# A forgetting-attention layer on one core: transposes of q, k and p moved from TensorE to VectorE and ScalarE

## The chip, the cores and the metric

The kernel runs on one core of a Trainium2 chip, in one launch. The metric is the device time of an execution in microseconds (us). An execution's time is a little longer than the span that the profile shows, since something lies before the first and after the last profiled instruction.

Engine names as in the profile: PE is TensorE's matmul, PEld its weight load, DVE VectorE, ACT ScalarE, POOL GpSimd, SP the engine that issues the large DMAs.

## What is computed

One layer, of the kind that the reference calls FoX (a softmax attention with a cumulated forget gate instead of positions), and a gated feed-forward network with a causal convolution of width 3 behind it. The sequence has 256 positions, the model 2048 columns, there are 16 heads of 128, and the feed-forward part has 2 x 5632 columns. Everything is float32. Cut to what matters here:

```python
def fox_mixer(h, w_in, b_f, q_gain, k_gain, w_out):
    q, k, v, f_logit = jnp.split(h @ w_in, [hd, 2 * hd, 3 * hd], axis=-1)
    q = rms_norm(q.reshape(bsz, seq, N_HEADS, HEAD_DIM), q_gain)
    k = rms_norm(k.reshape(bsz, seq, N_HEADS, HEAD_DIM), k_gain)
...
    cum = jnp.cumsum(log_sigmoid(f_logit + b_f), axis=1).transpose(0, 2, 1)
    s = jnp.einsum('bqhd,bshd->bhqs', qb, k) * HEAD_DIM ** -0.5
    s = s + (cq[..., :, None] - cum[:, :, None, :])
    return _causal_softmax(s, start, v)          # then @ w_out

h = h + fox_mixer(rms_norm(h, mix_norm), ...)
h = h + conv_ffn(rms_norm(h, ffn_norm), w_up, conv_w, conv_b, w_down)
```

## The kernel before

**Tiles.** The 256 positions are two tiles of 128 (t), the 2048 model columns 16 k-tiles of 128. Every large product is made of three matmuls per k-tile and t: each operand is split into a high part (hi), which is a cast to the reduced type fp32r, and a low part (lo), the rest; hi*hi, hi*lo and lo*hi are summed (L324 to L326). A matmul of this kind has 512 columns.

**Weights.** `split_load` (L159) brings four k-tiles of 512 columns (1 MB) in one DMA from SP into one of 4 raw buffers; then for each half of it (two k-tiles, 1024 columns) ACT casts the hi tile (L169) and DVE subtracts to make the lo tile (L170). hi and lo have HBUF = 5 buffers each, so a cast can start only when PE has read the tile five before it for the last time. Two k-tiles feed 12 matmuls.

**Attention.** The heads are worked in four groups of four (GROUPS, heads 12 to 15 first). For each group g the chunks q, k and v are made one after the other (`chunk`, L308; in group 0 v is made in two pieces, v0a, which also carries the forget gate's 16 columns, and v0b). Behind a q or k chunk ACT moves the two banks to SBUF with the row's scale (`qk_evac`), DVE squares and sums per head and POOL takes the power -0.5, DVE scales each head (`qk_norm`, L409). Then q and k must be turned, so that the 128 columns of a head lie on the partitions: `qk_turn` (L414) does it with PE, by matmuls against an identity, four 128x128 squares into a bank of PSUM, and ACT copies the bank to SBUF with the gain per partition (L425), into T0 (q) and T1 (k).

**Scores and output of a head.** `scores` (L435) makes the bias on POOL from the cumulated gate (which comes over DRAM, `scr` to `ckB`), two matmuls (sc), adds the bias and takes the maximum on DVE, exponentials with sums on ACT (L463), reciprocal and two scalings on DVE (L469). The result s is p, 128 x 384 per head: positions 0 to 127 see 128 keys, positions 128 to 255 see 256. `turn_p` (L474) turns its three squares with PE (pp, L477) and DVE copies them to pT (L479). `mix_v` (L482) multiplies v with pT into a bank po, ACT casts the hi half os from it and DVE subtracts the lo half.

**What sets the order.** Steps that belong behind a chunk are put into a queue of functions, `bg`; `tick()` takes one from it after every second k-tile of the next chunks. `attend_steps` (L500) hands out one step per tick: in step i the scores of head i, the turn of p of head i - LAG_P (3), the product with v of head i - LAG_V (5). A scheduler then puts the instructions of each engine into one fixed order, and each engine works its own order from the front; an instruction that waits holds all that stand behind it on its engine. After the four groups comes the output projection (`out_part`), whose rows of os it needs, group by group, and the addition to the residual (`out_evac`, L293), whose result is turned again for the feed-forward part (`h_turn`, two steps for each of four column blocks).

Of the kernel before, what the change touches and what calls it, by code (L numbers as in the profile page):

```python
# [9 lines left out]
F32 = mybir.dt.float32  # L10
# [6 lines left out]
S = 256  # L17
NT = S // P
# [11 lines left out]
LAG_P = 3  # L30
LAG_V = 5
# [64 lines left out]
def trunk_kernel(  # L96
# [193 lines left out]
    def out_evac(pts, c):  # L290
        for t in range(NT):
            hc = res[:, t, c * 512 : (c + 1) * 512]
            nc.vector.tensor_tensor(hc, hc, pts[t], op=ALU.add)  # L293
            sq = hp_.tile([P, 512], F32, tag="hsq", name=f"hsq{c}_{t}")
            square(sq, t, c)
        bg.extend([
            nop,
            (lambda kp=2 * c: h_turn(kp)),
            (lambda kp=2 * c + 1: h_turn(kp)),
        ])  # L300

    with tc.tile_pool(name="att", bufs=2) as att, tc.tile_pool(name="ckp", bufs=1) as ckp:
# [110 lines left out]

        def qk_turn(sb, i, nh, grp):  # L414
            tT = att.tile([P, 4, S], F32, tag=f"T{i}", name=f"T{i}_{grp}", bufs=1)

            def pair(hp, w):
                pt = bank(f"pT{i}_{grp}_{hp}")
                for h in range(w):
                    for t in range(NT):  # L420
                        nc.tensor.transpose(
                            pt[:, h * S + t * P : h * S + (t + 1) * P],
                            sb[:, t, (hp + h) * HD : (hp + h + 1) * HD], ident,
                        )
                nc.scalar.activation(  # L425
                    tT[:, hp : hp + w, :],
                    pt[:, 0 : w * S].rearrange("p (h s) -> p h s", s=S),
                    AF.Copy, scale=gqk[i],
                )

            return tT, [
                (lambda hp=hp: pair(hp, min(2, nh - hp))) for hp in range(0, nh, 2)
            ]

        def scores(hh, h, qT, kT, ckB):  # L435
# [17 lines left out]
            s = att.tile([P, 3 * P], F32, tag="s", name=f"s{hh}", bufs=4)  # L453
# [18 lines left out]
            return s  # L472

        def turn_p(hh, s):  # L474
            pp = bank(f"pp{hh}")
            for i in range(3):
                nc.tensor.transpose(pp[:, i * P : (i + 1) * P], s[:, i * P : (i + 1) * P], ident)  # L477
            pT = att.tile([P, 3 * P], F32, tag="pT", name=f"pT{hh}")
            nc.vector.tensor_copy(pT, pp[:, 0 : 3 * P])  # L479
            return pT  # L480

        def mix_v(hh, h, pT, vsb):  # L482
            po = bank(f"po{hh}")
# [15 lines left out]

        def attend_steps(g, h0, nh, qT, kT, vsb):  # L500
            st = {}

            def step(i):
                if i == 0:
                    st["ckB"] = ckB = att.tile([P, 4, S], F32, tag="ckB", name=f"ckB{g}", bufs=1)
                    nc.gpsimd.dma_start(
                        ckB[:, 0:nh, :].rearrange("p h s -> p (h s)"),
                        scr[h0 : h0 + nh, :].rearrange("h s -> (h s)").unsqueeze(0).to_broadcast([P, nh * S]),
                    )
                    return  # L510
                i -= 1
                if 0 <= i - LAG_V < nh:
                    h = i - LAG_V
                    mix_v(h0 + h, h, st["p", h], vsb)
                if 0 <= i - LAG_P < nh:
                    h = i - LAG_P
                    st["p", h] = turn_p(h0 + h, st["s", h])
                if i < nh:
                    st["s", i] = scores(h0 + i, i, qT, kT, st["ckB"])

            return [(lambda i=i: step(i)) for i in range(nh + LAG_V + 1)]

        for g, (h0, nh) in enumerate(GROUPS):
            qd = {}

            def q_done():
# [3 lines left out]
                bg.extend([nop] * max(0, 3 - len(bg)))  # L530
# [32 lines left out]
            bg.extend([nop] * 3)  # L563
# [190 lines left out]
```

## Time and profile before

| what | value |
|---|---|
| median of three timed executions | 1133.18 us (1133.14 to 1133.82) |
| the profiled execution, its own time | 1132.92 us |
| span of that execution in the profile | 1131.2 us |
| PE busy | 1124.5 us, 99% of the span |
| PEld busy | 962.1 us, 85% |
| DVE busy | 737.0 us, 65% |
| ACT busy | 580.4 us, 51% |
| POOL busy | 53.1 us, 5% |
| granted clock of PE, mean | 1.00 |

Busy time counts each moment in which at least one instruction of the engine is under way. Matmuls are pipelined: the next one starts before the one ahead has ended, so the mean duration of one (391 ns for 512 columns) is longer than its share of the time. The time that one really takes is read from rows of the chain, where a run of them has a start and a length. The first transpose of q starts at 57 us of the span and the last po at 333; what follows is the output projection and, for two thirds of the span, the feed-forward part, which the change does not touch but for `h_turn`.

### The profile page before, as it was taken

The numbers are of one execution on the slowest core, as the hardware profiler recorded it, in microseconds if no ns is written. First come the engines' busy times: TensorE is split into PE (matmuls) and PEld (weight loads), VectorE is DVE, ScalarE is ACT, GpSimd is POOL, SyncE is SP. The second block draws the span as 40 slices with busy tenths as digits, with TensorE's granted clock in tenths as the row PEclk, the third lists the DMA queues.
The fourth block names the chain that finished last, engine by engine and source line by source line (L and its number), as shares of the span: only waits on it lengthen the run. The fifth ranks groups of instructions, "written<-read, shape, count | busy, mean of one in ns | idle before, by whom it ended". The sixth has DMA issues, their size and how long they took to land.

```text
span 1131.2 us, 14984 instructions
## 1 busy us (share of the span) xinstructions
PE 1124.5 (99%) x5796; PEld 962.1 (85%) x5796; DVE 737.0 (65%) x1189; ACT 580.4 (51%) x853; POOL 53.1 (5%) x102
## 2 busy tenths in 40 slices
PE   9999999999999999999999999999999999999998
PEld 6898888888888888888888888888888888888886
DVE  7667556566556557777755777775577767547864
ACT  7655454454445456555434555543465554345542
POOL 0104011030100000000000000000000000000000
PEclk9999999999999999999999999999999999999999
DMA  9765454554545555555555555555555555555552
GB/s 345 293 204 207 157 197 154 182 198 156 186 155 186 186 178 184 197 187 186 191 200 183 183 204 192 187 186 193 184 187 198 194 193 193 188 185 186 191 182 75
DMA packets 33543, 215.23 MB, mean 190 GB/s; under 512 B 3824, under 2 KB 4112, under 8 KB 9152
## 3 DMA queue, kind: packets, MB, share of 16 engines
q1 hardware_dynamic: 32624, 211.96, 54.3%
q0 software_dynamic: 704, 2.30, 0.6%
q8 instruction: 45, 0.74, 0.3%
q14 instruction: 26, 0.21, 0.1%
q10 hardware_dynamic: 144, 0.02, 0.0%
HBM read 212.15 MB, written 2.11 MB: 189 GB/s over the span
## 4 chain that ended last, share of the span: by engine, by line
PE 99%; DMA 0%; DVE 0%; SPq 0%; ACT 0%; issue 0%
PE puv L265 14%; PE pug L265 14%; PE puv L267 7%; PE pug L267 7%; PE pd L276 7%; PE pd L278 7%; PE pd L277 7%; PE pk L324 3%; PE pk L326 3%; PE po L276 3%; PE po L278 3%; PE pk L325 3%; PE po L277 3%; PE pq L325 3%; PE pq L326 2%; PE pq L324 2%
## 5 line engine op out<-in xcount | busy, mean ns | idle before, releaser
L265 PE MATMUL pug<-hs,hi_ug 128*128 128x512 f32 x704 | 168.1, 391 | 0.0
L265 PE MATMUL puv<-hs,hi_uv 128*128 128x512 f32 x704 | 167.9, 391 | 0.0
L170 DVE TENSOR_TENSOR lo_ug<-raw_ug,hi_ug 128x1024 fp32r<-128x1024 f32 x88 | 106.0, 1221 | 84.3 <-PE puv L267 39.3
L170 DVE TENSOR_TENSOR lo_d<-raw_d,hi_d 128x1024 fp32r<-128x1024 f32 x88 | 106.6, 1222 | 78.7 <-ACT hi_d L169 56.1
L169 ACT CAST hi_d<-raw_d 128x1024 fp32r<-128x1024 f32 x88 | 92.2, 1052 | 114.8 <-PE pd L278 83.1
L265 PEld LDWEIGHTS pug<-hs,hi_ug 128*128 128x128 f32 x704 | 129.6, 188 | 25.3
L265 PEld LDWEIGHTS puv<-hs,hi_uv 128*128 128x128 f32 x704 | 129.4, 188 | 25.0
L169 ACT CAST hi_ug<-raw_ug 128x1024 fp32r<-128x1024 f32 x88 | 92.5, 1051 | 109.7 <-PE puv L265 37.9
L169 ACT CAST hi_uv<-raw_uv 128x1024 fp32r<-128x1024 f32 x88 | 92.5, 1051 | 100.2 <-PE pug L265 64.0
L170 DVE TENSOR_TENSOR lo_uv<-raw_uv,hi_uv 128x1024 fp32r<-128x1024 f32 x88 | 106.2, 1220 | 57.4 <-PE pug L267 40.6
L277 PE MATMUL pd<-lo_d,gt 128*128 128x512 f32 x352 | 136.2, 389 | 0.0
L276 PE MATMUL pd<-hi_d,gt 128*128 128x512 f32 x352 | 134.5, 389 | 0.0
L278 PE MATMUL pd<-hi_d,gt 128*128 128x512 f32 x352 | 134.2, 389 | 0.0
L267 PEld LDWEIGHTS pug<-hs,lo_ug 128*128 128x128 f32 x704 | 90.3, 191 | 3.4
L267 PEld LDWEIGHTS puv<-hs,lo_uv 128*128 128x128 f32 x704 | 90.3, 191 | 3.4
L267 PE MATMUL puv<-hs,lo_uv 128*128 128x256 f32 x704 | 91.3, 283 | 0.0
L267 PE MATMUL pug<-hs,lo_ug 128*128 128x256 f32 x704 | 91.3, 283 | 0.0
L278 PEld LDWEIGHTS pd<-hi_d,gt 128*128 128x128 f32 x352 | 66.1, 188 | 13.8
L276 PEld LDWEIGHTS pd<-hi_d,gt 128*128 128x128 f32 x352 | 66.1, 188 | 13.6
L277 PEld LDWEIGHTS pd<-lo_d,gt 128*128 128x128 f32 x352 | 66.1, 188 | 13.6
L170 DVE TENSOR_TENSOR lo_o<-raw_o,hi_o 128x1024 fp32r<-128x1024 f32 x32 | 39.2, 1224 | 31.2 <-ACT hi_o L169 31.2
L170 DVE TENSOR_TENSOR lo_q<-raw_q,hi_q 128x1024 fp32r<-128x1024 f32 (+1 forms) x33 | 39.3, 1192 | 28.8 <-ACT hi_q L169 28.7
(169 smaller groups left out, 1820.0 us busy)
## 6 DMA issues: line engine op xcount, KB each, us to landing
raw_ug<-in_w_up SPq DMA_DIRECT2D x44, 1024.0 KB, 4.9
raw_uv<-in_w_up SPq DMA_DIRECT2D x44, 1024.0 KB, 4.9
raw_d<-in_w_down SPq DMA_DIRECT2D x44, 1024.0 KB, 4.9
raw_k<-in_w_in SPq DMA_DIRECT2D x16, 1024.0 KB, 4.9
raw_o<-in_w_out SPq DMA_DIRECT2D x16, 1024.0 KB, 4.9
raw_q<-in_w_in SPq DMA_DIRECT2D x12, 1024.0 KB, 4.9
raw_v<-in_w_in SPq DMA_DIRECT2D x12, 1024.0 KB, 4.8
raw_q<-in_w_in SPq DMA_DIRECT2D x7, 512.0 KB, 6.7
```

The costliest lines, as they stand in the source:

```text
L169: nc.scalar.copy(hi[:, 0 : w * n], src)
L170: nc.vector.tensor_tensor(lo[:, 0 : w * n], src, hi[:, 0 : w * n].bitcast(F32), op=ALU.subtract)
L265: nc.tensor.matmul(o[:, 0:512], lhsT=hv, rhs=a.rearrange("p a s -> p (a s)"), start=first, stop=False)
L267: nc.tensor.matmul(o[:, 0:S], lhsT=lv, rhs=a[:, 0, :], start=False, stop=last)
L276: nc.tensor.matmul(pts[t], lhsT=ah, rhs=hv, start=first, stop=False)
L277: nc.tensor.matmul(pts[t], lhsT=ah, rhs=lv, start=False, stop=False)
L278: nc.tensor.matmul(pts[t], lhsT=al, rhs=hv, start=False, stop=last)
L324: nc.tensor.matmul(o, lhsT=ah, rhs=hv[j], start=(k == 0), stop=False)
L325: nc.tensor.matmul(o, lhsT=ah, rhs=lv[j], start=False, stop=False)
L326: nc.tensor.matmul(o, lhsT=al, rhs=hv[j], start=False, stop=(k == KT - 1))
```

## The change

The line numbers shift by a few.

- **q and k.** The transposes on PE and the copy of a bank are gone. `squares` turns each 128x512 half of q or k in place, in squares of 32x32, with one DVE instruction (STREAM_TRANSPOSE, L419): after it, each square is turned, but still lies in the quarter of the partitions in which it lay before. `move(d)` brings the squares to their places: for each quarter d of the result four ACT copies (L425), one from each quarter o of the partitions, each of 32 partitions by 2 x 4 x 32 elements, with the gain as before. That makes 2 DVE and 16 ACT instructions for a q or k of a group, in five steps of the queue; before there were 16 matmuls and 2 ACT copies of 128x512, in two steps.
- **p.** The transposes on PE and DVE's copy of 128x384 are gone. `turn_p` turns the p of all four heads together, for quarter o of the rows and quarter d of the columns in one STREAM_TRANSPOSE on DVE that reads 32 partitions and writes 32 others (L474, 12 squares of 32x32): 16 instructions for a group, in four steps.
- **The order.** Attention goes by stage: one step fetches the gate's sums, one makes the scores of all four heads, four turn p, and one multiplies all four heads with v. The p and pT of a group are one tile each. A bank po is shared by two heads. The empty steps (`nop`) ahead of the turns go, others come into `attend_steps`. `h_turn` does two of its pieces in one tick.

```diff
...
@@ -295,8 +294,7 @@
             square(sq, t, c)
         bg.extend([
             nop,
-            (lambda kp=2 * c: h_turn(kp)),
-            (lambda kp=2 * c + 1: h_turn(kp)),
+            (lambda c=c: [h_turn(kp) for kp in (2 * c, 2 * c + 1)]),
         ])
 
     with tc.tile_pool(name="att", bufs=2) as att, tc.tile_pool(name="ckp", bufs=1) as ckp:
@@ -411,28 +409,27 @@
                         ss[:, t, h : h + 1], None, op0=ALU.mult,
                     )
 
+
         def qk_turn(sb, i, nh, grp):
             tT = att.tile([P, 4, S], F32, tag=f"T{i}", name=f"T{i}_{grp}", bufs=1)
 
...
+            def squares():
+                for t in range(NT):
+                    b = sb[:, t, 0 : nh * HD]
+                    nc.vector.transpose(b, b)
+
+            def move(d):
+                out = tT[d * SQ : (d + 1) * SQ, 0:nh, :].rearrange("p h (t s) -> p t h s", t=NT)
+                for o in range(P // SQ):
+                    src = sb[o * SQ : (o + 1) * SQ, :, 0 : nh * HD].rearrange("p t (h d) -> p t h d", d=HD)
+                    nc.scalar.activation(
+                        out[:, :, :, o * SQ : (o + 1) * SQ], src[:, :, :, d * SQ : (d + 1) * SQ],
+                        AF.Copy, scale=gqk[i][d * SQ : (d + 1) * SQ],
+                    )
+
+            return tT, [squares] + [(lambda d=d: move(d)) for d in range(P // SQ)]
+
+        def scores(hh, h, qT, kT, ckB, sg):
             bias = att.tile([P, 3 * P], F32, tag="bias", name=f"bias{hh}")
             nc.gpsimd.tensor_scalar(
                 bias[:, 0:P], ckB[:, h, 0:P], -1.0, cum[:, 0, hh : hh + 1],
@@ -450,7 +447,7 @@
             sc = bank(f"sc{hh}")
             nc.tensor.matmul(sc[:, 0:P], lhsT=qT[:, h, 0:P], rhs=kT[:, h, 0:P], start=True, stop=True)
             nc.tensor.matmul(sc[:, P : 3 * P], lhsT=qT[:, h, P:S], rhs=kT[:, h, :], start=True, stop=True)
-            s = att.tile([P, 3 * P], F32, tag="s", name=f"s{hh}", bufs=4)
+            s = sg[:, h, :]
             st = att.tile([P, 4], F32, tag="st", name=f"st{hh}", bufs=4)
             segs = ((0, P), (P, 3 * P))
             for i, (a, b) in enumerate(segs):
@@ -469,18 +466,17 @@
                 nc.vector.tensor_scalar(
                     s[:, a:b], s[:, a:b], st[:, 2 + i : 3 + i], None, op0=ALU.mult
                 )
-            return s
-
...
+        def turn_p(sg, pg, nh, d):
+            src = sg[:, 0:nh, :].rearrange("p h (m s) -> p (h m) s", s=P)
+            dst = pg[:, 0:nh, :].rearrange("p h (m s) -> p (h m) s", s=P)
+            for o in range(P // SQ):
+                nc.vector.transpose(
+                    dst[d * SQ : (d + 1) * SQ, :, o * SQ : (o + 1) * SQ],
+                    src[o * SQ : (o + 1) * SQ, :, d * SQ : (d + 1) * SQ],
+                )
+
+        def mix_v(hh, h, pT, vsb, po):
             nc.tensor.matmul(
                 po[:, 0:S], lhsT=vsb[:, 0, h * HD : (h + 1) * HD], rhs=pT[:, 0:S],
                 start=True, stop=False,
@@ -497,28 +493,39 @@
                 os_[hh][:, 1, :], po[:, 0:S], os_[hh][:, 0, :].bitcast(F32), op=ALU.subtract
             )
 
+
         def attend_steps(g, h0, nh, qT, kT, vsb):
             st = {}
...
+            hs_ = range(nh)
+
+            def fetch():
+                st["ckB"] = ckB = att.tile([P, 4, S], F32, tag="ckB", name=f"ckB{g}", bufs=1)
+                nc.gpsimd.dma_start(
+                    ckB[:, 0:nh, :].rearrange("p h s -> p (h s)"),
+                    scr[h0 : h0 + nh, :].rearrange("h s -> (h s)").unsqueeze(0).to_broadcast([P, nh * S]),
+                )
+
+            def step_s():
+                st["s"] = att.tile([P, 4, 3 * P], F32, tag="s", name=f"s{g}", bufs=1)
+                for h in hs_:
+                    scores(h0 + h, h, qT, kT, st["ckB"], st["s"])
+
+            def step_p(d):
+                if d == 0:
+                    st["p"] = att.tile([P, 4, 3 * P], F32, tag="pT", name=f"pT{g}", bufs=1)
+                turn_p(st["s"], st["p"], nh, d)
+
+            def step_v():
+                for h in hs_:
+                    if h % 2 == 0:
+                        pair = bank(f"po{h0 + h}")
+                    mix_v(h0 + h, h, st["p"][:, h, :], vsb, pair[:, h % 2 * S : (h % 2 + 1) * S])
+
+            return (
+                [fetch, nop, step_s, nop] + [nop] * (g < len(GROUPS) - 1)
+                + [(lambda d=d: step_p(d)) for d in range(P // SQ)]
+                + [step_v]
+            )
 
         for g, (h0, nh) in enumerate(GROUPS):
             qd = {}
@@ -527,7 +534,6 @@
                 qsb = qk_evac(qd["p"], nh, "q")
                 qk_norm(qsb, 0, nh, g)
                 qd["T"], turns = qk_turn(qsb, 0, nh, g)
-                bg.extend([nop] * max(0, 3 - len(bg)))
                 bg.extend(turns)
 
 
@@ -560,7 +566,6 @@
             ksb = qk_evac(pk, nh, "k")
             qk_norm(ksb, 1, nh, g)
             kT, turns = qk_turn(ksb, 1, nh, g)
-            bg.extend([nop] * 3)
             bg.extend(turns)
             if g == 0:
                 pv = chunk("v0a")
```

The scheduler makes new orders of this. Names in the rows below: hi_k_1_2 is the hi tile of the second half of k's second block, s_929 or st_930 the p and the sums of a head (s_951 is now that of the group), T_1 is T of group 1, po, pv and pk are banks.

ACT of before, from the cast of group 1's first k block on; the exponentials (L463) are those of group 0's first three heads:

```order
L169 CAST hi_k_0_0_1110<-raw_k_0_1108 128x1024
L463 ACT_TABLE_LOAD
L463 ACTIVATE s_929,st_930<-s_929,st_930 128x128
L463 ACTIVATE s_929,st_930<-s_929,st_930 128x256
L169 CAST hi_k_0_2_1114<-raw_k_0_1108 128x1024
L463 ACTIVATE s_973,st_974<-s_973,st_974 128x128
L463 ACTIVATE s_973,st_974<-s_973,st_974 128x256
L169 CAST hi_k_1_0_1167<-raw_k_1_1165 128x1024
```

ACT of the changed kernel, where the same exponentials (now L460) stand:

```order
L168 CAST hi_v_0_0_1317<-raw_v_0_1315 128x1024
L460 ACT_TABLE_LOAD
L460 ACTIVATE s_951,st_964<-s_951,st_964 128x128
L460 ACTIVATE s_951,st_964<-s_951,st_964 128x256
L425 ACTIVATE T_1_1107<-qsb,gq 32x2x4x32 x5
L460 ACTIVATE s_951,st_985<-s_951,st_985 128x128
L460 ACTIVATE s_951,st_985<-s_951,st_985 128x256
L425 ACTIVATE T_1_1107<-qsb,gq 32x2x4x32 x7
L168 CAST hi_v_0_2_1321<-raw_v_0_1315 128x1024
L425 ACTIVATE T_1_1107<-qsb,gq 32x2x4x32 x2
L460 ACTIVATE s_951,st_1006<-s_951,st_1006 128x128
L460 ACTIVATE s_951,st_1006<-s_951,st_1006 128x256
```

The exponentials stood one block of k apart from each other; now those of all four heads (the fourth's follow at once) stand in group 1's v chunk, eight casts later, with 14 moves of q between them.

On DVE the copy L479 of each head, which stood between other pieces of work, has become 16 STREAM_TRANSPOSE in a row behind the fourth head's scaling; the lo tile of v's second block stands behind them.

PE of before, the second head's po and the fourth head's transposes, in group 1's k chunk:

```order
L326 MATMUL pk_1_1107<-hi_k_0_2_1114,xs_97 128x512
L484 MATMUL po_1154<-pT_1083,vsb 128x256
L488 MATMUL po_1154<-pT_1083,vsb 128x128
L477 MATMUL pp_1159<-ident,s_1057 128x128 x3
L324 MATMUL pk_0_1106<-hi_k_1_0_1167,xs_98 128x512
```

PE of the changed kernel, the first po of group 0, in group 1's v chunk:

```order
L322 MATMUL pv_0_1313<-hi_v_1_0_1357,xs_98 128x512
L322 MATMUL pv_1_1314<-hi_v_1_0_1357,xs_98 128x512
L480 MATMUL po_1190<-pT_1082,vsb 128x256
L484 MATMUL po_1190<-pT_1082,vsb 128x128
L480 MATMUL po_1200<-pT_1082,vsb 128x256
L484 MATMUL po_1200<-pT_1082,vsb 128x128
L323 MATMUL pv_0_1313<-lo_v_1_0_1358,xs_98 128x512
```

The products with v went from one head at a time in the k chunk to heads 12 and 14 together in the v chunk; the other two heads of the group follow 34 matmuls later, into the same two banks. No transposes are left between them.

## Rows read from the trace of the kernel before

**Rows 1.** The page, parts 1 and 4: busy time; chain that ended last.

```profile
PE 1124.5 (99%) x5796; PEld 962.1 (85%) x5796; DVE 737.0 (65%) x1189; ACT 580.4 (51%) x853; POOL 53.1 (5%) x102
...
PE 99%; DMA 0%; DVE 0%; SPq 0%; ACT 0%; issue 0%
```

**Rows 2.** Waits of PE: line waited for, us in total, times, longest.

```profile
PE pq L324 <- ACT hi_q L169: 0.9, 2, 0.5
```

**Rows 3.** One window: length, busy PE, PEld, DVE, ACT, POOL (count), granted clock, DMA share, GB/s.

```profile
60.00:140.00 80.00, 80.00 (x440) 69.45 (x439) 53.02 (x112) 41.90 (x65) 16.15 (x29) 1.00 0.55 188
```

**Rows 4.** Chain of waits, two pieces: start, length, engine, tile, line, count.

```profile
58.28 0.66 PE pT L421 x6
...
414.61 3.65 PE pug L265 x16
```

**Rows 5.** Groups of PE by shape: out<-in, count | busy us, mean ns | idle before.

```profile
L265 PE MATMUL pug<-hs,hi_ug 128*128 128x512 f32 x704 | 168.1, 391 | 0.0
...
L452 PE MATMUL sc<-T,T 128*128 128x256 f32 x32 | 9.6, 380 | 0.0
...
L477 PE MATMUL pp<-ident,s 128*128 128x128 f32 x48 | 7.8, 272 | 0.0
...
L421 PE MATMUL pT<-ident,ksb 128*128 128x128 f32 x32 | 5.3, 272 | 0.0
...
L209 PE MATMUL pw<-zeros 128*128 128x256 f32 x8 | 3.8, 651 | 1.3 <-DVE zeros L206 1.3
```

**Rows 6.** Groups of DVE by shape, columns as in rows 5.

```profile
L170 DVE TENSOR_TENSOR lo_v<-raw_v,hi_v 128x1024 fp32r<-128x1024 f32 x24 | 29.4, 1223 | 25.6 <-ACT hi_v L169 25.6
...
L479 DVE COPY pT<-pp 128x384 f32<-128x384 f32 x16 | 8.8, 553 | 6.6 <-PE pp L477 6.6
...
L409 DVE TENSOR_SCALAR qsb<-qsb,ss 128x128 f32<-128x128 f32 x32 | 6.6, 280 | 2.9 <-POOL ss L404 2.9
...
L293 DVE TENSOR_TENSOR res<-res,po 128x512 f32<-128x512 f32 x8 | 5.1, 679 | 0.0
```

**Rows 7.** Timeline of DVE: start, us, operation, count [idle before <- releaser].

```profile
92.12 0.17 DVE L467 RECIPROCAL st<-st 128x2 f32<-128x2 f32 x1 [1.05 <-ACT s L463]
...
92.79 0.28 DVE L457 CUSTOM_DVE_ANT_0 s<-sc,bias 128x128 f32<-128x128 f32 x1
...
111.80 0.42 DVE L496 TENSOR_TENSOR os<-po,os 128x256 fp32r<-128x256 f32 x1
112.13 1.06 DVE L409 TENSOR_SCALAR qsb<-qsb,ss 128x128 f32<-128x128 f32 x5
```

**Rows 8.** Timeline of ACT, the first head's exponentials.

```profile
88.44 1.05 ACT L169 CAST hi_k<-raw_k 128x1024 fp32r<-128x1024 f32 x1 [1.66 <-PE pq L326]
89.50 1.28 ACT L463 ACT_TABLE_LOAD   x1
91.11 0.40 ACT L463 ACTIVATE s<-s,st 128x128 f32<-128x128 f32 x1 [0.32 <-DVE st L461]
...
91.51 0.49 ACT L463 ACTIVATE s<-s,st 128x256 f32<-128x256 f32 x1
...
92.00 1.03 ACT L169 CAST hi_k<-raw_k 128x1024 fp32r<-128x1024 f32 x1
```

**Rows 9.** Timeline of ACT, the first stretch.

```profile
3.23 0.51 ACT L212 ACTIVATE xs<-xq,gains 128x256 fp32r<-128x256 f32 x1 [0.51 <-DMA gains<-in_cols]
...
15.77 2.50 ACT L212 ACTIVATE xs<-xq,gains 128x256 fp32r<-128x256 f32 x6
...
23.15 2.00 ACT L169 CAST hi_k<-raw_k 128x1024 fp32r<-128x1024 f32 x2 [1.42 <-DMA raw_k<-in_w_in]
```

**Rows 10.** Groups of ACT by shape, columns as in rows 5.

```profile
L495 ACT CAST os<-po 128x256 fp32r<-128x256 f32 x16 | 5.9, 367 | 0.0
```

**Rows 11.** Timeline of POOL, from the gate's sums to the second head's mask.

```profile
78.45 0.57 POOL L374 DMA_DIRECT2D scr<-cumT  x1 [18.50 <-DVE cumT L373]
...
91.65 0.53 POOL L446 TENSOR_SCALAR_AFFINE_SELECT bias<-bias 128x128 f32<-128x128 f32 x2
```

More of the change, by code (lines that the diff above doesn't have):

```diff
@@ L17 @@
 S = 256
+SQ = 32
 NT = S // P
@@ L29 @@
 HBUF = 5
-LAG_P = 3
-LAG_V = 5
 GROUPS = [(12, 4), (8, 4), (4, 4), (0, 4)]
@@ L415, in qk_turn @@
             tT = att.tile([P, 4, S], F32, tag=f"T{i}", name=f"T{i}_{grp}", bufs=1)
[L417 to L435, printed above, removed]
+            def squares():
[12 more added lines that the diff above has]
+        def scores(hh, h, qT, kT, ckB, sg):
             bias = att.tile([P, 3 * P], F32, tag="bias", name=f"bias{hh}")
@@ L471, in scores @@
                 )
-            return s
[L474 to L483, printed above, removed]
+        def turn_p(sg, pg, nh, d):
[7 more added lines that the diff above has]
+        def mix_v(hh, h, pT, vsb, po):
             nc.tensor.matmul(
@@ L501, in attend_steps @@
             st = {}
[L503 to L521, printed above, removed]
+            hs_ = range(nh)
[23 more added lines that the diff above has]
+            )
         for g, (h0, nh) in enumerate(GROUPS):
```

## The prediction

> **What bounds the kernel now.** I read the page first: TensorE (PE) is busy 1124.5 of 1131.2 us, and the chain of work that ended last is 99% PE [rows 1]. Then PE's own waits: the largest for another engine's result in attention is 0.9 us in all, for hi halves of q's weights [rows 2]. Then a window of 80 us in which attention runs: PE is busy 80.00 of it at a granted clock of 1.00, which is the 2.4 GHz level, while VectorE (DVE) is busy 53.0 and ScalarE (ACT) 41.9 [rows 3]. So PE's instructions set the time, the other two have 27 and 38 us free in these 80, and whatever leaves PE is won, as long as PE is not made to wait instead. That second half is the whole question, because a free third of an engine says nothing about one late result. The profiled execution took 1132.92 us, 0.26 under the median of 1133.18; I sum against 1132.92.
>
> **What leaves PE.** A transpose has a mean duration of 272 ns, but matmuls overlap; what counts is its pitch on the chain. Six in a row held the chain 0.66 us, so 0.11 each [rows 4]. Of p there are 48, of k 32, and of q 32 of the same kind [rows 5]: 112 x 0.11 = **12.3 us** off the path. From the same view, a 512-column matmul has a pitch of 3.65/16 = 0.228 [rows 4], which I use to count PE's lead.
>
> **What the other engines get.** DVE loses 16 copies of 553 ns [rows 6] and gets 16 transposes of 128x512 and 64 of 32x12x32. ACT loses 16 activations of 128x512 and gets 128 moves of 256 elements on 32 partitions.
> *A move.* The trace has the same operation (a copy with a pointer scale, 256 elements) on 128 partitions: alone 0.51, six in a row 2.50, so (2.50 - 0.50)/5 = 0.40 [rows 9]. I take 0.41. Below it lies the 256-element cast at 0.37 [rows 10], above it 0.51, if no move overlaps the one before.
> *A p transpose.* 384 elements per partition: the nearest row is the 128x384 copy at 0.55 [rows 6]. Five scalings of 128x128 in a row took 1.06 [rows 7] with 0.28 each [rows 6], so a successor starts 0.085 early when nothing holds it; that would give 0.47. These 16 change their 32 input partitions each time, and no row shows such a pair, so I take the full 0.55. Bounds: 0.33, the pitch of a 256-element operation (111.80 to 112.13, [rows 7]), and 0.68, that of a 512-element one [rows 6].
> The Trainium skill ("VectorE: DVE Perf Modes", section "Two Vector instructions with no wait between them") says that an instruction whose start quadrant differs from its predecessor's starts only when that one has finished; no row of before shows it; by it the pitch is the full duration, and where the rule didn't hold, the sum below would be 16 x 0.08 = 1.3 us lower. The table of the same page's section "The three transpose paths" counsels TensorE for 128x128 and gives VectorE only 32x32 blocks; that speaks against this change, but here TensorE is the engine that is full.
>
> In sum a group of four heads gives DVE about 4 x 0.68 + 16 x 0.55 - 4 x 0.55 = 9.3 us and ACT 32 x 0.41 - 4 x 0.69 = 10.4. A group lasts three chunks of 96 matmuls, 66 us, in which by the shares of [rows 3] some 22 us of DVE and 31 of ACT are free: on the average it is hidden. What is not hidden are lumps at fixed places in in-order queues.
>
> **The place that decides: the first output of group 0.** In the changed order PE reaches the first po (p times v of heads 12 and 14) in group 1's v block. The p transposes must be done by then, and they stand behind all four heads' softmax, which stands behind the exponentials on ACT, and between these the moves of group 1's q are queued. I count both sides from one event, the last matmul on the hi tile of k's second block, whose buffer the cast of v's first block waits for:
> - PE from there to po: 75 matmuls x 0.228 = 17.1 us.
> - ACT: that matmul's end 0.39 [rows 5]; cast 0.95 (two took 2.00 with 1.05 each, [rows 9]); table load 1.28; four heads' exponentials, 0.89 a head (91.11 to 92.00, [rows 8]) = 3.56; 14 moves x 0.41 = 5.74; one more cast 0.95. Sum 12.87.
> - DVE: 0.12 until the reciprocal starts (92.00 to 92.12), 0.67 for it and two scalings (92.12 to 92.79, [rows 7]), then 16 x 0.55 = 8.8. Sum 9.6.
> Together 22.5, so PE waits **5.4 us**. With the low bounds (0.37, 0.33) it is 1.4, with the high ones (0.51, 0.68) 8.9. In before nothing like it arises: each head's transposes stood one or two blocks behind its softmax, and each head was taken apart. Queued behind the waiting po are the rest of v's matmuls, and with them the hi and lo buffers; ACT and DVE run ahead meanwhile, so the wait isn't paid twice.
> There is a second way to the same po. POOL keeps its instructions, but the gate's sums (pcumT) now stand late in group 1's q chunk, and POOL takes them in order: 13.7 us from their DMA to the second head's mask [rows 11], with the power for group 1's q between the masks now. I walked all queues in order with these durations: from pcumT on, this way takes 37.5 us against 32.3 us of PE's work, a wait of 5.2 at the same po. It is the same wait, not a second one; but a quicker ACT alone would not take it away.
>
> **Two smaller waits.** Ahead of the second cast of group 1's q block (hi_q_0_2) ACT now has all 32 moves of group 0's q and k: 32 x 0.41 = 13.1, with four casts (3.8), v's evacuations and the gate's functions (about 1.0), the cast itself and its lo (1.1 + 1.2) and 0.4 for the hand-overs, 20.6 against 20.3 of PE's work since the last matmul of v0a's late block: **0.3**. In the output projection the first matmul of column block 2 waits for the addition into res of block 0, which DVE has put behind a lo tile: 0.4 for the matmul's end, 1.1 for the cast, 1.15 for lo, 0.7 for the addition [rows 6] = 3.4, against 11 matmuls of lead, 2.5: **0.9**.
>
> **Edits that I cost at nothing.** In groups 1 to 3 the four exponentials and the p transposes have no moves between them that come so late, and an in-order walk through all queues with these durations leaves no wait there. A po bank is now shared by two heads, so the second head's po waits for the first's subtraction. Its cover: 34 matmuls x 0.228 = 7.8 us, against a 0.37 cast [rows 10], a 0.42 subtraction [rows 7] and at most two lo tiles of 1.22 before it [rows 6], 3.2; in the last group it is 18 matmuls, 4.1 us. Two steps of the FFN transposes in one tick move four transposes, and the sums of the gates come some blocks later; PE's count stays.
>
> **Sum:** 1132.92 - 12.3 + 5.4 + 0.3 + 0.9 = 1127.2, so **1127 us**, faster by 0.5%.
>
> **Rivals.**
> *A. Nothing overlaps (slower).* Mechanism: each move pays its full 0.51 and each transpose 0.58, because each starts on other partitions than the one before. Place: the same first po, 7.2 (+1.8); hi_q_0_2, 32 x 0.10 = 3.2 later, 3.3 - 0.2 for what PE lost just before (+2.9); the second lo tile of group 2's k block, behind q's p transposes and squares (+1.7); the second block of group 2's v (+1.8); and small ones at the po of groups 2 and 3 (+2.1). Together 10.3: **1137.5**. It decides from a move of 0.49 on, with the transposes at 0.55: the walk gives -2.5 against before at 0.47 and +0.8 at 0.50. For it: the pitch of 0.40 is known only for moves on the same 128 partitions. Against it: casts that change buffer each time overlap too, by 0.10 (2.00 for two of 1.05, [rows 9]).
> *B. All of it is hidden.* If the transposes run at 0.33 and the moves at 0.37, first po costs 0 to 1.4 and the rest 0.9: 1132.92 - 12.3 + 0.9 (+1.4) = **1121.5 to 1122.9**. For it: the free time in [rows 3]; and casts that stand waiting for PE (1.66 us ahead of the cast at 88.44, [rows 8]), so ACT has no backlog. Against it: that wait is for the same buffers that I count from.
> *C. PE's clock falls behind the wait of 5.4.* Before, PE never waited that long in attention, and the granted clock there is 1.00 [rows 2, 3]. The eight warm-up matmuls that follow PE's idle start have a mean of 651 ns against 380 for the same shape later [rows 5]: 8 x 0.27 = 2.2 us. So **1129.4**. The Trainium skill ("TensorE: Matmul & The Clock Gate", section "HAM oscillation — how this bites in real kernels") says that idle gaps of PE put its clock back to 1.2 GHz and that the work behind them runs slow. In [rows 3] the clock is 1.00 and PE has no idle gap, so no row here shows it.
> *D. The transposes stay on PE.* The changed order has none of q, k or p on PE; 0.01.
>
> **How the numbers follow.** Forecast 0.47 (1123 to 1131, its own range), A 0.26 with what lies between it and the forecast at 0.13, B 0.08, C 0.05. This kernel's measurement tells about 0.2%, 2.3 us, from no change: 1130.9 to 1135.5 is the same. Faster: the forecast, B and C, 0.60. Same: what lies between, 0.13. Slower: A and D, 0.27. Range: from 1122, where a tenth (most of B) lies below, to 1139, since A's centre must lie in it; beyond is the case of transposes at 0.68 and moves at 0.51 together (walk: +11, 1144), about a tenth.
>
> **What would show each step.** No pp and no pT on PE and PE busy about 12 us less: the saving. A wait of PE for the p transposes at one place, about 131 us into the span, of 4 to 7 us, first in the list of PE's waits: the deciding place; under 1.5, B. Durations: a lump of 15 moves about 6.2 us long, and 16 p transposes 8.8; 7.7 and more of moves with a wait at hi_q_0_2 of 2 us and more would be A. A granted clock under 1.00 behind the wait: C. I am wrong if PE waits in groups 2 to 4 as it does in group 0, if a wait for a po bank appears, or if casts come late for another reason than the moves.

## The result and the profile after

The changed kernel takes 1144.85 us (median of 4, 1144.66 to 1145.73) against 1133.36 (1133.14 to 1133.82): a ratio of 1.0102, 95% interval 1.009 to 1.0114. It is slower by 11.5 us, where 6 us faster was forecast, and above the forecast range. The profiled execution took 1144.66 us, its span is 1142.9.

The page after, busy time and the chain, to be read against [rows 1], and PE's granted clock in 40 slices of the span:

```profile
PE 1116.5 (98%) x5684; PEld 952.3 (83%) x5684; DVE 771.7 (68%) x1253; ACT 632.1 (55%) x965; POOL 55.2 (5%) x102
...
PEclk9999899999999999999999999999999999999999
...
PE 79%; DVE 10%; ACT 6%; issue 3%; POOL 1%; DMA 1%; SPq 0%; POOLq 0%; ACTq 0%; DVEq 0%
```

112 matmuls have left PE (48 of p, and 8 for each q or k of a group; the 16 named under the change is twice too many) and its busy time has fallen by 8.0 us. But its idle time has risen from 1131.2 - 1124.5 = 6.7 to 26.4, by 19.7, and 19.7 - 8.0 = 11.7 is the difference of the spans. A fifth of the chain now runs outside PE. PE's waits after (against [rows 2]: engine, tile and line <- what it waited for: us in total, times, longest):

```profile
PE po L480 <- DVE pT L474: 12.1, 3, 7.3
PE pq L322 <- ACT hi_q L168: 3.7, 3, 2.3
PE pv L322 <- ACT hi_v L168: 2.1, 2, 1.5
...
PE pq L323 <- DVE lo_q L169: 1.1, 2, 0.5
PE pk L323 <- DVE lo_k L169: 0.8, 1, 0.8
PE pv L323 <- DVE lo_v L169: 0.5, 1, 0.5
PE po L480 <- DVE os L492: 0.4, 1, 0.4
PE pv0b L323 <- DVE lo_v0b L169: 0.4, 1, 0.4
```

Without the start of the program these are eleven waits, 19.2 us. In order of time: lo_v0b 0.42; hi_q 2.33 and lo_q 0.53 in group 1's first q block; hi_v 0.55, and 7.29 for pT at group 0's first po; lo_k 0.77 in group 2; 2.54 for pT in group 2; hi_v 1.54 and lo_v 0.53; 2.24 for pT in group 3, and 0.44 for a po bank. The durations of the new operations (p transposes and moves; line, engine, shapes, count | busy, mean ns | idle before):

```profile
L474 DVE STREAM_TRANSPOSE pT<-s 32x384 f32<-32x384 f32 x64 | 36.4, 569 | 0.9
L425 ACT ACTIVATE T<-ksb,gains 32x256 f32<-32x256 f32 x64 | 32.4, 506 | 7.5 <-DVE ksb L419 6.7
```

And their lumps on the timelines of ACT and DVE, with the gate's second function (`fe`) behind the moves of k:

```profile
59.80 8.29 ACT L425 ACTIVATE T<-qsb,gq 32x256 f32<-32x256 f32 x16
...
71.81 8.27 ACT L425 ACTIVATE T<-ksb,gains 32x256 f32<-32x256 f32 x16
80.11 0.23 ACT L341 ACTIVATE fe<-fe 128x32 f32<-128x32 f32 x1
...
123.02 3.62 ACT L425 ACTIVATE T<-qsb,gq 32x256 f32<-32x256 f32 x7
...
130.88 0.55 DVE L466 TENSOR_SCALAR s<-s,st 128x128 f32<-128x128 f32 x2
131.47 9.32 DVE L474 STREAM_TRANSPOSE pT<-s 32x384 f32<-32x384 f32 x16
```

Sixteen moves take 8.29: from one start to the next (8.29 - 0.51)/15 = 0.52, with no overlap. Sixteen p transposes take 9.32, 0.583 each; they start behind the scaling of the fourth head (130.88). Behind the first po's wait, on PE's timeline and in windows (columns as in [rows 3]); the two lines from 269.44 on are the same work in group 2, behind a wait of 2.54 us:

```profile
140.84 1.22 PE L480 MATMUL po<-pT,vsb 128*128 128x256 f32 x2 [7.29 <-DVE pT L474]
...
143.42 0.77 PE L323 MATMUL pv<-lo_v,xs 128*128 128x512 f32 x1
...
145.69 0.39 PE L323 MATMUL pv<-lo_v,xs 128*128 128x512 f32 x1
...
269.44 0.70 PE L480 MATMUL po<-pT,vsb 128*128 128x256 f32 x2 [2.54 <-DVE pT L474]
...
270.77 0.47 PE L323 MATMUL pk<-lo_k,xs 128*128 128x512 f32 x1
...
135.00:140.00 5.00, 0.00 (x0) 0.00 (x0) 4.89 (x9) 2.70 (x3) 0.00 (x0) 0.54 0.00 0
140.00:145.00 5.00, 4.16 (x12) 3.51 (x13) 4.96 (x7) 0.75 (x2) 0.00 (x0) 0.50 0.19 28
145.00:150.00 5.00, 5.00 (x22) 4.07 (x21) 5.00 (x7) 1.28 (x2) 0.00 (x0) 0.93 0.98 380
```

The clock is granted at 0.50, the 1.2 GHz level, until about 145.5: the four pairs of matmuls into po took 2.58 us (140.84 to 143.42) and the five matmuls of v behind them 2.27 (to 145.69). In group 2, at a granted clock of 1.00, the four pairs took 1.33 (269.44 to 270.77), and five matmuls of v at 0.228 are 1.14. So the clock costs 2.4 us.

### The profile page after: what moved, and what is told of

Same layout as the page of the kernel before. It is cut to its first block, busy times and chain, and to the rows that moved or that the text cites. A ratio compares the mean times of both kernels' runs of the same rounds, so it can differ in the third digit from the quotient of the medians.

```text
span 1142.9 us, 14925 instructions
## 1 busy us (share of the span) xinstructions
PE 1116.5 (98%) x5684; PEld 952.3 (83%) x5684; DVE 771.7 (68%) x1253; ACT 632.1 (55%) x965; POOL 55.2 (5%) x102
## 4 chain that ended last, share of the span: by engine, by line
PE 79%; DVE 10%; ACT 6%; issue 3%; POOL 1%; DMA 1%; SPq 0%; POOLq 0%; ACTq 0%; DVEq 0%
PE puv L264 14%; PE pug L264 14%; PE puv L266 7%; PE pug L266 7%; PE pd L276 7%; PE pd L275 7%; PE pd L277 7%; ACT T L425 4%; DVE pT L474 3%; PE po L277 2%; PE po L275 2%; PE po L276 2%; DVE lo_o L169 1%; PE pk L323 1%; PE pk L324 1%
```

## The experiments

Each was timed beside the kernel before, whose medians in the four batches were 1133.59, 1133.7, 1133.55 and 1133.55. The theory at this point (L): the moves on ACT, each without overlap, delay what stands behind them in ACT's order. The rivals: the p transposes alone (P), and the order by stage (S).

**q and k back on PE.**

```diff
...
-            return tT, [squares] + [(lambda d=d: move(d)) for d in range(P // SQ)]
...
+            return tT, [
+                (lambda hp=hp: pair(hp, min(2, nh - hp))) for hp in range(0, nh, 2)
+            ]
...
```

> The changed kernel with q and k turned on PE again (and ACT's two copies per tensor, and the empty steps ahead of them); p stays on DVE, attention by stage. Theory L (lumps: what PE waits for are the 128 moves on ACT, which delay casts and exponentials; the p transposes alone find cover): PE's waits in attention all but vanish, none over 1 us, the granted clock is 1.00 throughout, and the time is that of before less 48 transposes of p, 1133.2 - 48 x 0.11 = 1127.9, between 1127 and 1129. Rival P (the 16 p transposes in a row are too long by themselves): a wait of 4 us and more for pT at group 0's first po stays, with the slow clock behind it, and the time is 1134 or more. Rival S (attention by stage is what costs, wherever the turning is done): several waits of 1 to 3 us at po, 1135 or more.

Measured: 1126.93, ratio 0.9942 (0.9925 to 0.9958). All of PE's waits:

```profile
PE pq L322 <- ACT hi_q L168: 1.4, 2, 0.9
PE pw L208 <- DVE zeros L205: 1.3, 1, 1.3
PE pq L323 <- DVE lo_q L169: 0.5, 1, 0.5
```

P falls: the p transposes, still 569 ns each, are fully covered (every wait listed is one of the program's start), and this part alone gains 6.7 us. Part of the cover seems to come from the gate, though no run changes that alone: the gate's logarithm (Ln) starts at 70.91, where it starts at 87.11 in the changed kernel behind the lump at 71.81, so the scores start 9 us earlier (91.5 instead of 100.4) and the first po stands at 113.6 instead of 140.8.

**p back on PE.**

```diff
...
-                nc.vector.transpose(
-                    dst[d * SQ : (d + 1) * SQ, :, o * SQ : (o + 1) * SQ],
...
+            for i in range(3):
+                nc.tensor.transpose(pp[:, i * P : (i + 1) * P], sg[:, h, i * P : (i + 1) * P], ident)
+            nc.vector.tensor_copy(pg[:, h, :], pp[:, 0 : 3 * P])
...
```

> The changed kernel with p turned on PE again, three squares a head and DVE's copy, in the step order of the changed kernel; q and k stay on DVE and ACT. Theory L: the moves keep their 0.515 us each; so PE still waits 2 to 3 us for hi_q in group 1's first q block, and some 4 to 5 us at group 0's first po, now for the copies of pT. 1133.2 - 64 x 0.11 + 8.4 of waits + about 1 for restarting = 1135.6, and up to 2.4 more if PE's clock falls behind the longer wait: 1135 to 1138. Rival P: without the p transposes nothing is late, 1133.2 - 7.0 = 1126 to 1128.

Measured: 1131.9, ratio 0.9987 (0.9978 to 0.9997), under L's range and above P's. The waits at hi_q (2.33), lo_q (0.53) and lo_v0b (0.44) came as expected; the 4 to 5 us at the first po did not:

```profile
PE pq L322 <- ACT hi_q L168: 2.8, 2, 2.3
...
PE pq L323 <- DVE lo_q L169: 1.1, 2, 0.5
PE pv0b L323 <- DVE lo_v0b L169: 0.4, 1, 0.4
```

My count had let the first po wait for all four heads. With a copy per head it waits only for its own: the first two heads' copies start at 130.35, before the third head's scaling, and po at 134.44. In the changed kernel each of the 16 instructions holds a piece of all four heads. So theory L is too narrow: the q and k part alone gains 1.7 (of the 7.0 of its 64 transposes, since 3.3 us of waits stay and the clock falls behind them, to 0.57 in the window 82:86), the p part alone gains 6.7, and both together lose 11.5. Neither alone makes the first po wait. Together the moves push the softmax late, and the p transposes wait for the last head of it. Transposing p head by head on DVE, which would test the second half of that by itself, was not tried.

**Attention by stage with all turning on PE** (both edits above together).

> All of the turning back on PE (q, k and p, with the copies and the empty steps of before), but attention by stage for four heads, two heads to a po bank and two pieces of the FFN transposes in a tick, as in the changed kernel. Theory L: the order by stage costs nothing by itself, PE's waits are those of before, 1133.4 within 1. Rival S: the order by stage carries part of the loss, po waits of 1 us and more, 1136 or more.

Measured: 1133.2, ratio 0.9995 (0.9986 to 1.0005), with no wait behind the program's start, as in before. S falls, and with it the two pieces of `h_turn` in one tick as a cause.

**Same quarter.**

```diff
-                    src = sb[o * SQ : (o + 1) * SQ, :, 0 : nh * HD].rearrange(...)
+                    src = sb[d * SQ : (d + 1) * SQ, :, 0 : nh * HD].rearrange(...)
...
-                    src[o * SQ : (o + 1) * SQ, :, d * SQ : (d + 1) * SQ],
+                    src[d * SQ : (d + 1) * SQ, :, o * SQ : (o + 1) * SQ],
```

> The changed kernel, but each move and each p transpose reads the quarter of the partitions that it writes, instead of another one; so q, k and p are not rightly turned, and everything else is as it was. Four instructions in a row now read and write the same 32 partitions, and only every fourth changes them. Theory Q (an instruction that starts on other partitions than its predecessor can't overlap it): a lump of 16 moves falls from 8.3 us to 12 x 0.41 + 4 x 0.515 = 7.0, a lump of 16 p transposes from 9.3 to 12 x 0.49 + 4 x 0.58 = 8.2; the wait at group 0's first po falls from 7.3 to about 4.8, the one at hi_q nearly vanishes, and the time to 1128 to 1134. Rival F (the form costs it: 32 partitions in runs of 32 elements, whatever the partitions): 8.3 and 9.3 stay, and the time is 1144 to 1146.

Measured: 1128.49, ratio 0.9956 (0.9941 to 0.997). The lumps on ACT and DVE, and PE's wait at the first po:

```profile
59.46 6.84 ACT L425 ACTIVATE T<-qsb,gq 32x256 f32<-32x256 f32 x16
...
127.20 7.84 DVE L474 STREAM_TRANSPOSE pT<-s 32x384 f32<-32x384 f32 x16
...
135.10 1.22 PE L480 MATMUL po<-pT,vsb 128*128 128x256 f32 x2 [5.59 <-DVE pT L474]
```

Inside the two lumps, the third to the fifth instruction of each, one to a line; the fifth is the first on another quarter:

```profile
60.27 0.49 ACT L425 ACTIVATE T<-qsb,gq 32x256 f32<-32x256 f32 x1
60.67 0.49 ACT L425 ACTIVATE T<-qsb,gq 32x256 f32<-32x256 f32 x1
61.18 0.51 ACT L425 ACTIVATE T<-qsb,gq 32x256 f32<-32x256 f32 x1
...
128.17 0.52 DVE L474 STREAM_TRANSPOSE pT<-s 32x384 f32<-32x384 f32 x1
128.63 0.52 DVE L474 STREAM_TRANSPOSE pT<-s 32x384 f32<-32x384 f32 x1
129.16 0.57 DVE L474 STREAM_TRANSPOSE pT<-s 32x384 f32<-32x384 f32 x1
```

From start to start it is 0.40 inside a quarter and 0.51 into the next one on ACT, 0.46 and 0.53 on DVE. With 0.51 for the three steps that change the quarter, the other twelve moves have a mean pitch of (6.84 - 0.49 - 3 x 0.51)/12 = 0.40, the value that I had taken for all; the p transposes go to (7.84 - 0.53 - 3 x 0.54)/12 = 0.47. So on ACT the form costs nothing beside the 128-partition copy of [rows 9], and a change of partitions costs 0.10 to 0.12 per instruction on both engines. The change is enough by itself: here no instruction reads one quarter and writes another, and the three steps are held all the same. The order of PE's instructions is the same, and 1.5 us off each lump takes 16.4 us off the kernel: all waits in groups 1 to 3 are gone, and of those before only 5.59 and 0.53 are left. The first po's wait fell less than expected (to 5.59, not 4.8).

**Loops exchanged.**

```diff
-                for o in range(P // SQ):
+                o = d
+                for d in range(P // SQ):
...
```

> The changed kernel with the two loops of quarters exchanged, for the moves and for the p transposes: four instructions in a row now read the same 32 partitions and write different ones, where before they wrote the same and read different ones. Theory Q, in its wider form (a change on either side holds the next instruction back): the lumps stay at 8.3 and 9.3 us, PE's waits and the time stay, 1144 to 1146. Narrower form (only a change of the partitions read matters): lumps of 7.0 and 8.2, the time 1128 to 1130 as where neither changed.

Measured: 1146.27, ratio 1.0111 (1.0096 to 1.0126), lumps of 8.29 and 9.32 as before the exchange, and nearly the same waits (7.29 at the first po). It is 1.4 us slower than the change although its waits in attention are shorter (17.8 us in all, against 19.2): the clock falls behind a wait of 2.59 too (0.50 in the window 271:274) and in group 1's first q block (0.53 in 83:86), and PE is busy 1119.8 us instead of 1116.5. On DVE a change of the partitions written holds the next instruction back as one of those read does; on ACT too, though there the gain's partitions, which are read, change with those written. No order of these sixteen pieces avoids both.

**A later po.**

```diff
-                [fetch, nop, step_s, nop] + [nop] * (g < len(GROUPS) - 1)
+                [fetch, nop, step_s, nop] + [nop] * ((9 if g == 0 else 1 + 0) if g < len(GROUPS) - 1 else 0)
```

> The changed kernel with eight more empty steps ahead of group 0's p transposes, so that on PE its first po stands 24 matmuls (5.5 us) later in group 1's v chunk, with ACT's and DVE's lumps where they were. Theory B (the lump itself is in the way: behind the 16 p transposes on DVE stands the lo tile that PE needs next, so a later po only moves the wait to that tile): PE waits about 6 us for lo_v instead of 7.3 for pT, and the time stays within 2 us of the changed kernel's, 1142.5 to 1146. Rival W (only the place of po is wrong): the long wait is gone with the slow clock behind it, 9 to 10 us less, 1134 to 1136.

Measured: 1148.78, ratio 1.0137 (1.0122 to 1.0152), more than either expected. DVE's lump and what PE waits for instead:

```profile
132.32 6.97 DVE L474 STREAM_TRANSPOSE pT<-s 32x384 f32<-32x384 f32 x12
139.32 1.23 DVE L169 TENSOR_TENSOR lo_v<-raw_v,hi_v 128x1024 fp32r<-128x1024 f32 x1
...
140.60 0.80 PE L323 MATMUL pv<-lo_v,xs 128*128 128x512 f32 x1 [7.07 <-DVE lo_v L169]
...
82.00:84.00 2.00, 1.81 (x4) 1.49 (x5) 2.00 (x3) 2.00 (x4) 0.00 (x0) 0.50 0.37 66
...
342.00:346.00 4.00, 4.00 (x12) 3.35 (x13) 4.00 (x4) 0.75 (x2) 0.00 (x0) 0.50 0.50 137
```

W falls: with po out of the way PE waits 7.07 us for the lo tile that stands behind the lump. The other steps moved as well, and PE waits 3.38 for pT in group 1 and 4.43 in group 3. But its waits in attention come to 18.8 us in all, no more than the 19.2 of the change. What makes it slower still is the clock: it is at 0.50 behind four waits (2.32, 7.07, 3.38 and 4.43) instead of one, and PE is busy 1121.7 us instead of 1116.5 with as many matmuls.

**One tensor at a time.** In the first of these k alone is on PE, in the second q alone.

```diff
...
+        def qk_turn(sb, i, nh, grp):
+            return (qk_turn_pe if i == 1 else qk_turn_v)(sb, i, nh, grp)
...
```

> The changed kernel with k alone turned on PE; q's moves stay on ACT, p on DVE. Theory L, by place: without k's 16 moves the gate's functions and hi_q_0_2 on ACT aren't late, so the waits of 2.3 and 0.5 us in group 1's first q block vanish; q's 14 moves still stand between the exponentials of group 0, so a wait for pT of about 3 us stays at its first po (shorter than 7.3, since the scores come earlier), the rest under 1. 1133.4 - 80 x 0.11 + 3.2 + 0.4 + 0.3 = 1128.5, 1127.5 to 1131. If q's moves don't matter there, 1125.

> The changed kernel with q alone turned on PE; k's moves stay on ACT, p on DVE. Theory L, by place: with no moves between the exponentials of group 0 its first po is not waited for; k's lump of 16 finds cover by itself; no wait over 1 us. 1133.4 - 80 x 0.11 + 0.8 = 1125.4, 1124 to 1126.5, under every kernel so far. If any lump of moves beside the p transposes is too much, a wait of 2 us or more for a cast or for pT stays, 1128 or more.

Measured: 1129.86 with k on PE, ratio 0.9964 (0.9951 to 0.9977), and 1127.28 with q on PE, 0.9944 (0.9929 to 0.9959). The first po with k on PE, and the one larger wait with q on PE:

```profile
127.69 1.22 PE L504 MATMUL po<-pT,vsb 128*128 128x256 f32 x2 [3.02 <-DVE pT L498]
```

```profile
PE pk L323 <- DVE lo_k L169: 2.0, 1, 2.0
```

By place it is as expected: q's moves between the exponentials make the first po late (3.02 of 3.2), and without them nothing waits there. The waits at hi_q in group 1 go in both, since one lump of 16 ahead of it is covered. q on PE missed its range by 0.8 us: it waits 2.0 for lo_k where 0.8 was counted for all waits.

**The moves on POOL.** First all, then k's alone with q on PE.

```diff
-                    nc.scalar.activation(
+                    nc.gpsimd.tensor_scalar(
                         out[:, :, :, o * SQ : (o + 1) * SQ], src[:, :, :, d * SQ : (d + 1) * SQ],
-                        AF.Copy, scale=gqk[i][d * SQ : (d + 1) * SQ],
+                        gqk[i][d * SQ : (d + 1) * SQ], None, op0=ALU.mult,
                     )
```

> The changed kernel with the 128 moves on POOL instead of ACT (a multiplication by the gain per partition, same pieces); POOL was busy 55 us of the span. Theory L: what PE waited for came from ACT's lumps, so with the p transposes alone nothing is late by more than 2 us, and the time is 1133.4 - 12.3 plus 0 to 4 = 1121 to 1125, if a move takes about 0.48 there, as POOL's multiplication of 128x256 does. Rival O (a lump is a lump, on any in-order engine): POOL's moves stand ahead of the bias and the power of the heads, scores or p come late by 3 us and more, and the time is 1128 or more.

> q turned on PE, k by squares on DVE with its 64 moves on POOL, p on DVE. Theory L: as with q alone on PE, without the 2.0 us for lo_k in group 2's k block where that came from ACT's or DVE's queue behind k's moves: 1133.4 - 8.8 to 9.8, 1123.5 to 1126. Rival O: T of k comes late to the scores by 3 us and more, 1128 or more.

Measured: 1158.82, ratio 1.0219 (1.0204 to 1.0235), and 1133.96, 1.0007 (0.9997 to 1.0016). POOL's timeline and PE's waits with all moves there:

```profile
58.58 20.72 POOL L425 TENSOR_SCALAR T<-qsb,gq 32x256 f32<-32x256 f32 x14 [4.68 <-DVE qsb L419]
...
PE sc L448 <- POOL T L425: 14.8, 4, 5.0
PE po L480 <- DVE pT L474: 12.3, 2, 11.7
```

A move takes 1.3 to 1.4 us there on the mean, not 0.48: fourteen in 20.7. ACT's lumps are gone, and so is every wait for hi but the start's (0.8), as theory L has it; but T is late to the scores, and the last group's p with it. Rival O holds: a lump on a free engine is still a lump.

With k's moves alone on POOL the time is in rival O's range, but not by O's mechanism:

```profile
65.27 23.29 POOL L425 TENSOR_SCALAR T<-ksb,gains 32x256 f32<-32x256 f32 x16 [4.70 <-DVE fz L334]
88.62 0.59 POOL L372 DMA_DIRECT2D scr<-cumT  x1
...
PE po L504 <- DVE pT L498: 6.5, 1, 6.5
```

T itself is waited for 0.5 us in all. What comes late is the gate: POOL issues its DMA at 88.62, behind the 16 moves, where it stood at 78.45 in before [rows 11]. So DVE idles 8.8 us for group 0's first bias, and group 0's first po waits 6.5 us for pT, with the clock at 0.50 behind it (121:123).

**A version that beats both.** q on PE everywhere; k on PE in group 1 alone, or in group 0 alone.

> p on DVE, q on PE, k by squares and moves in groups 0, 2 and 3, and on PE in group 1. Theory L, by place: the wait of 2.0 us for lo_k in group 2's k block, the one larger wait left with q alone on PE, goes with the other order there; 72 transposes less: 1133.5 - 72 x 0.11 = 1125.6, 1124.5 to 1127. If that wait stays, 1128.

> p on DVE, q on PE, k by squares and moves in groups 1 to 3, and on PE in group 0, where the gate's functions stand on ACT behind k's moves. Theory L, by place: scores of group 0 come as early as where q and k are both on PE, no wait over 1 us, 1133.5 - 72 x 0.11 = 1125.6, 1124.5 to 1127. If a lump of k's moves costs in any group, a wait of 2 us and more and 1128.

Measured: 1125.52, ratio 0.9927 (0.9913 to 0.9942), and 1124.58, ratio 0.9923 (0.9906 to 0.9939). The second one's waits, all of them:

```profile
PE pw L208 <- DVE zeros L205: 1.3, 1, 1.3
PE pq L322 <- ACT hi_q L168: 0.9, 2, 0.5
PE pq L323 <- DVE lo_q L169: 0.5, 1, 0.5
PE po L504 <- DVE pT L498: 0.3, 1, 0.3
```

It is 9.0 us faster than before and 20.3 faster than the change, with 72 of the 112 transposes off PE and 0.3 us of new waits (the other three lines are the program's start).

## Why the prediction was wrong

**What leaves PE: right.** With the other 40 left and no new waits, 72 transposes brought 9.0 us, 0.125 each (0.10 to 0.15 by the interval), against the 0.11 that I took. At 0.11 each, the 12.3 us of all 112 were there to be won.

**The move: the step that failed.** I took 0.41, from six copies in a row on the same 128 partitions [rows 9]; it is 0.52, which makes the 14 moves on the way to the first po 1.5 us longer and every lump of 16 by 1.8. For the p transposes I had asked whether a change of partitions holds the next instruction back and taken the full 0.55 (measured 0.583); for the moves, which change partitions as often, I did not ask, and left it to rival A. The same-quarter run shows that 0.40 is right for moves that stay, and the exchanged loops that turning the change to the other side doesn't help. For DVE this agrees with the rule that I cited from the Trainium skill ("VectorE: DVE Perf Modes", section "Two Vector instructions with no wait between them"): 0.47 where nothing changes, 0.54 to 0.58 where it does. The same-quarter run, with 0.40 for most moves and 0.47 for most p transposes, has 5.59 at the first po, nothing in groups 1 to 3, and takes 1128.49: about the forecast with rival C's clock (1129.4). That is in part luck, since its lump of p transposes is 1.0 us shorter than the 8.8 that I took; but at that pitch the path holds. No run changes the pitch of the moves alone, so what the p transposes' 0.583 adds in groups 1 to 3 stays open.

**The deciding place: right place, wrong size.** PE waits at group 0's first po, for pT, from 133.6 to 140.8 us into the span, behind the chain that I counted: 7.29 us, where rival A had 7.2 and the forecast 5.4. (By its own terms the forecast's bounds there are 1.3 and 8.8, not 1.4 and 8.9.)

**The smaller waits.** hi_q and its lo in group 1's first q block: 0.3 forecast, 3.3 in A, measured 2.33 + 0.53. The output projection's 0.9 did not come at all, and 0.42 for lo_v0b and 0.55 for hi_v came that neither the forecast nor A had counted. In groups 1 to 3, behind those places, I had counted nothing, and A some 5.6; measured were 0.77, 2.54, 1.54 + 0.53, 2.24 and 0.44, 8.1 in all. This is the largest part of the miss, and the 0.44 is the wait for a po bank that I had named as a sign of being wrong. In these groups the lumps only just exceed their cover, as the same-quarter run shows: 1.5 us off each lump, and all 8.1 are gone.

**Rivals taken one at a time.** A (1137.5) has its mechanism, and C too: 2.4 us for the clock behind the long wait, where 2.2 was priced. But C was priced beside the forecast alone and A without C, although A's wait at the same po is the longer one. Together they give 1139.7. What is still missing is 5 us. 2.3 are waits: 19.2 instead of the 6.6 + 10.3 = 16.9 of A. About 1.3 are the restart, which I did not price: the first matmul or pair behind a wait takes 0.11 to 0.12 longer than in a row (0.50 for 0.39, 0.70 for 0.59), eleven times. The clock's 2.4 for 2.2 is 0.2 more. The remaining 1.2 us I can't assign.

**The range.** It ended at 1139, between A and the case of both high bounds, which I had put at 1144 with a tenth. It should have reached A and C together with the high bounds, some 1146.

**Clock.** The Trainium skill ("TensorE: Matmul & The Clock Gate", section "HAM oscillation — how this bites in real kernels") says that idle gaps put PE's clock back to 1.2 GHz; the windows above agree, 0.54 in the wait and 0.50 behind it. Shorter waits did so too in other runs, and not each time: 0.57 behind 3.02 with k on PE (127:131), 0.57 behind 2.33 and 0.53 with p on PE (82:86), and 0.50 behind 2.59 with the loops exchanged; but in the changed kernel it is 1.00 behind the same 2.33 and 0.53 (81:87) and behind 2.54 (269:275). What decides between these is open.

## What to carry to other kernels

Where one engine is full and the others have a third of their time free, work can leave the full one for nothing only if its result has slack at its place: count from one event, along both engines, and ask for each in-order queue what now stands behind the lump. Two moves that each gain alone can lose together, because the second is late by what the first delays; here they gained 1.7 and 6.7 alone and lost 11.5 as a pair. Take a pitch only from instructions that also share the partitions of the ones that you price, and add rivals that bring each other on.

## What the runs showed of the hardware

- On ACT as on DVE an instruction whose 32 partitions differ from those of its predecessor does not overlap it: 0.51 to 0.52 for 0.40 on ACT, 0.54 to 0.58 for 0.47 on DVE. On DVE a change of those read alone and of those written alone each did it; on ACT the gain's partitions changed with those written.
- On POOL the same move of 32 partitions x 256 took 1.3 to 1.4 us on the mean, where a multiplication of 128x256 took 0.47 (at 86.52 in before). The pieces are runs of 32 elements with strides; whether these or the partitions cost it was not tried.
- PE's granted clock was 0.50 behind the 7.29 us wait for some 5 us, which cost 2.4 us. Behind waits of 2.3 to 2.6 us it fell in some runs and stayed at 1.00 in others.
- Behind a wait the first matmul or pair took 0.11 to 0.12 us longer than in a row (0.50 for 0.39, 0.70 for 0.59), with the clock at 1.00.
